# One hybrid-attention encoder layer on one core: the split of two heads' sum a step later, small loads moved up, later norms in halves, MLP squares stored a step later

## The chip, the cores and the metric

The kernel runs on one core of one Trainium2 chip. The core has five engines with an instruction stream each: TensorE (PE in the profile; its weight loads are listed as PEld), VectorE (DVE), ScalarE (ACT), GpSimd (POOL) and SyncE (SP), which here only issues DMAs. The metric is the device time of one execution in microseconds; three runs of the kernel before gave a median of 2637.62 us (2637.33 to 2642.32).

## The reference: what is computed

One layer, sequence 2048, width 1024, float32. Cut to what matters:

```python
mod = silu(c) @ w_ada + b_ada                      # six vectors of 1024: sh1 sc1 gt1 sh2 sc2 gt2
h = rmsnorm(x, g_norm1) * (1 + sc1) + sh1
q_sb, k_sb, v_sb, q_ca, k_ca, v_ca = split(h @ w_in)   # six pieces of 512 columns, 8 heads of 64 each
# stick-breaking attention (8 heads, strictly causal), z = q k / 8
w = sigmoid(z) * prod over the keys between s and t of (1 - sigmoid(z))     # from a running sum in the reference
o_sb = w @ v_sb
# chunked softmax attention (8 heads), own chunk of 64 and 8 chunks before it,
# q and k rms-normed per head, a learned relative bias
o_ca = softmax(q_ca k_ca / 8 + bias) @ v_ca
x = x + gt1 * (concat(o_sb, o_ca) @ w_o)
h = rmsnorm(x, g_norm2) * (1 + sc2) + sh2
x = x + gt2 * (square(relu(h @ w1)) @ w2)          # hidden width 4096
```

## The kernel before, in words

The sequence is reversed on the host and cut into four blocks of 512 tokens (`TB`); most tiles are 128 partitions by 512 float32. A product in full precision is made of two halves in a rounded format: every operand is split into a high part (ACT casts it) and a low part (DVE or POOL subtracts), and `mm3` issues three matmuls, high by high, high by low, low by high. Scratch tensors in DRAM (`scr_q`, `scr_k`, `scr_v`, `scr_w`, `scr_m`, `scr_hid`, `scr_s` and others) carry split operands from one stage to the next. Each engine runs its own instructions in the order in which the scheduler of the framework put them; most instructions go through a wrapper that keeps them in program order, and so have the line number of that wrapper, L42. SP's queue is in order as well: a store at its head that waits for a compute engine holds back the loads behind it.

**Start.** `load_x(3)`, the conditioning vector, the bias columns and `gcol[:, 0]` are loaded, then `load_first(k)` loads for each of eight k the three weight pieces (`wf`) and two rows of `w_ada` (`wa`). The loop `for k in range(KT)` prepares and multiplies k by k: the first three weight pieces by block 3, into six PSUM banks. After it the six results are stored (`store_qk`, tiles `stf`), and behind these stores come the loads of `gcol[:, 1]` (g_norm2) and of `gqk_sb` (the gains of the per-head norms).

**Projections.** `jobs` lists weight piece and block; `run_job` goes through its banks (8 times 3 matmuls each, tiles `pq` or `pt`) and calls `hook(job, n)` before each. The hooks do the norms of the other blocks: `start_norm` (squares and sums, then two later parts that make the rstd and multiply x, tile `xt`) and `end_norm(tb, ht)`, which for each of eight tiles adds the shift: ACT writes the high part of `ht`, DVE the low part. In hook ((0,3,3),1) DVE scales `gqk_sb` into `gqk_s`. Pieces 6 and 8 (q and k of the chunked heads) are normed per head: ACT squares a bank (`csq`), DVE reduces it (`cv`), POOL makes the power (`cy`), DVE scales the bank into `qh`, which frees the bank.

**Attention.** `units` lists (head, query block, key block) for the stick-breaking heads (class `SB`) and (head, query block) for the chunked heads (class `CA`), block 3 first, then 2, 1, 0, each block all SB heads and then all CA heads. A unit has four steps; the step loop runs with lag: the front unit's scores and weights at step i, the back unit's transposes and value products 8 steps (`LAG`) later. A step of an SB unit: PE makes `z`, ACT takes the sigmoid in place, DVE scans it into `p`, POOL subtracts neighbours into the weights `b`; the back unit's weights are transposed on PE (`wt`), split by ACT (`wth`) and DVE (`wtl`), and multiplied by `v` into `acc`. `z` and `wt` share four PSUM banks. `load(u)` brings q and k of a unit two units (`AHEAD`) before its first step, `load_values` its v. Two heads share one tile of 128 rows. At the end of a head `finish(u)` has ACT copy the two halves of `acc` into `otmp` and `o`; a list `soon` holds what is to be done one step later: `add`, in which POOL adds the halves, and after the second head of a pair, one more step later, `keep(u, o)`: ACT casts the sum `o` into the high part of `os`, POOL subtracts the low part, and SP stores `os` to `scr_m`.

Between the steps `fill` gives PE dense matmuls of a `Filler`: the projections that are still missing (`fill_qkv` for block 1, then 0; tiles `pf`, weights `fw` and `fv`), then the output projection (`outproj`, tiles `po`). A filler yields a float for a matmul, a callable for work on a finished bank, and "start" or "wait" once its first loads are issued; `RESTS` says for how many steps it then rests. The weight loads of the first filler are issued by its generator when the step loop first asks for work, after the last projection job.

**MLP.** Both products are made with seven instead of eight block products (Strassen-Winograd). `First` steps (7 products for each of 16 pairs of hidden tiles, of 12 matmuls each) form hidden tiles: relu and square on ACT, in `hidden` or, for product 2, in `run`, and each is stored at once to `scr_hid` by `keep(i, src)`; sums of squares (tiles `ca`, `cb`, `cv`, `ce`) are stored through `later.add(2, ...)`, two steps later. `second_sums` prepares sums of w2 (`w2s`, stored to `scr_s`). `Second` steps load pairs of hidden tiles and weights (`hw`), split them into `oph` and `opv`, and multiply.

Of the kernel before, what the change touches and what calls it, by code (L numbers as in the profile page):

```python
# [9 lines left out]
F32 = mybir.dt.float32  # L10
# [14 lines left out]
KT = D // P  # L25
# [54 lines left out]
def encoder_kernel(ctx, tc, xT, c, g1, g2, w_in, w_rest, gqk, bias, w_o, w1, w2, w_ada, b_ada, out):  # L80
    nc = tc.nc
    act, dve, pool, sp = nc.scalar, nc.vector, nc.gpsimd, nc.sync
    pe = Ordered(tc, nc.tensor)
    osp = Ordered(tc, nc.sync)
# [112 lines left out]
    def norm_apply(which, x, k, dst, pl, tg):  # L197

        j = 3 * which * KT + k
        a, b = aff[:, which, k : k + 1], mod[:, j : j + 1]  # L200
        hi, lo = dst[k][:, 0, :], dst[k][:, 1, :]
        act.activation(x, x, AF.Identity, scale=a, bias=b)
        act.copy(hi, x)
        return lambda: dve.tensor_tensor(lo, x, hi.bitcast(F32), op=ALU.subtract) and None
# [34 lines left out]
    if True:  # L239
# [228 lines left out]

            norms.add(wait, second)

        def end_norm(tb, ht):
            hts[tb] = ht
            for k, x in enumerate(xts[tb]):
                b = mod[:, k : k + 1]
                act.activation(ht[k][:, 0, :], x, AF.Identity, bias=b)
                dve.scalar_tensor_tensor(
                    ht[k][:, 1, :], x, b, ht[k][:, 0, :].bitcast(F32), op0=ALU.add, op1=ALU.subtract
                )
# [3 lines left out]
        def h_tile(tb):  # L482
            if tb % 2:
                return [hxp.tile([P, 2, TB], F32R, tag="hx", name=f"ht{tb}_{k}") for k in range(KT)]
            whole[tb] = hp.tile([P, KT, 2, TB], F32R, tag="hp", name=f"ht{tb}")
            return [whole[tb][:, k] for k in range(KT)]
# [10 lines left out]
        def load_first(k):  # L497
            if k % 2 == 0:
                wraw.append(ring.tile([P, 2, 3, CW], F32, tag="r8", name=f"wf{k}"))
            osp.dma_start(wraw[-1][:, k % 2], w_in[0:3, :, k, :].rearrange("g p c -> p g c"))  # L500
            for j in (KT + k, k):
                adas[j] = adaw.tile([P, D], F32, tag="wa", name=f"wa{j}")
                osp.dma_start(adas[j], w_ada[j * P : (j + 1) * P, :])
# [51 lines left out]
        for k in range(KT):  # L555
            if k + 2 < KT:
                load_first(k + 2)
            rest = norm_apply(0, xts[3][k], k, hts[3], np_, "a3") if k else None
            for j in (KT + k + 1, k + 1) if k + 1 < KT else ():
                ada_column(j, adas[j])  # L560
                if rest:
                    rest = rest()
            if rest:
                rest()
            if k + 1 < KT:
                first_scale(k + 1)
            if k + 2 < KT:
                first_w(k + 2)
            if k + 4 < KT:
                first_x(k + 4)  # L570
            if k == KT - 3:
                load_raw(*loads.pop(0), osp)
                load_x(2, osp)
            if k == KT - 1:
                for m in range(4):
                    weight_parts((0, 3), m)
            for m, p in enumerate(first):
                hi, lo = [w2s[k // 2][:, k % 2, l] if p == 2 else wide[:, k, l, p] for l in range(2)]
                for n in range(2):
                    cl = slice(n * P, (n + 1) * P)  # L580
                    mm3(
                        pss[2 * m + n], hi[:, cl], lo[:, cl], hts[3][k][:, 0, :], hts[3][k][:, 1, :],
                        k == 0, k == KT - 1,
                    )
# [3 lines left out]
        for m, p in enumerate(first):  # L588
            for n in range(2):
                grp, hf = divmod(p, 2)  # L590
                store_qk(grp, 0, pss[2 * m + n], stage(f"f{p}_3_{n}"), hf * 2 + n, 3)
        osp.dma_start(gcol[:, 1, :], g2)
        osp.dma_start(gqk_sb, gqk)

        todo = [(1.5, lambda j=j: ada(j)) for j in range(2 * KT, 6 * KT)]
        for i in range(NH):
# [5 lines left out]
        def hook(job, n):  # L602

            if (job, n) == ((0, 3, 3), 1):
                dve.tensor_scalar_mul(gqk_s[:, 0:1], gqk_sb[:, 0:1], 0.125)
                dve.tensor_copy(gqk_s[:, 1:2], gqk_sb[:, 1:2])
                for p in range(2):
                    sp.dma_start(scr_w[p,], wide[:, :, :, p, :].bitcast(F32))
            if (job, n) == ((0, 6, 3), 2):
                norms.flush()  # L610
                end_norm(2, h_tile(2))
            if (job, n) == ((0, 6, 2), 1):
                load_x(1)
            if (job, n) == ((0, 4, 3), 0):
                start_norm(1, 5, 3)
            if (job, n) == ((0, 10, 2), 0):
                norms.flush()
                end_norm(1, h_tile(1))
                load_x(0)
                behind.add(2, lambda: start_norm(0, 3, 2))  # L620
            if (job, n) == ((1, 6, 1), 2):
                norms.flush()
                end_norm(0, h_tile(0))
            if (job, n) == ((1, 6, 0), 1):
                sp.dma_start(scr_h, whole[0].bitcast(F32))

# [36 lines left out]
    if True:  # L663
# [36 lines left out]
        def finish(u):  # L700
            r = (u.h % 2) * HD
            q = HD - r
            if u.h % 2 == 0:
                pend["o"] = op.tile([P, TB], F32, tag="o", name=f"o{u.nm}")
            o = pend["o"]
            tmp = op.tile([P, TB], F32, tag="otmp", name=f"otmp{u.nm}")
            rows = slice(r, r + HD)
            act.copy(tmp[rows, :], u.acc[q : q + HD, :])
            act.copy(o[rows, :], u.acc[rows, :])

            def add():
                pool.tensor_tensor(o[rows, :], o[rows, :], tmp[rows, :], op=ALU.add)
                if u.h % 2:
                    soon.append(lambda: keep(u, o))

            soon.append(add)

# [187 lines left out]
            def weights(self, qi, kb):  # L905
                return self.ws[qi][:, (kb - qi) * P : (kb - qi + 1) * P]

        RESTS = {"wait": 4, "start": 3}
        resident = {}
        svs = []  # L910
        turn = [0]
# [39 lines left out]
        def fill_qkv(self, tb, ht, pieces):  # L951
# [3 lines left out]

            def narrow_load(piece, i):
                w = ring.tile([P, KT // 2, 2, CW], F32R, tag="r8", name=f"fw{tb}_{piece}_{i}")
                sp.dma_start(w.bitcast(F32), scr_w[piece,][:, i * 4 : i * 4 + 4, :, :])
                return {i * 4 + k: w[:, k] for k in range(KT // 2)}

            def wide_load(piece, k, n):
# [212 lines left out]
        AHEAD = 2  # L1174
        for u in units[:AHEAD]:
            load(u)
        run_job(len(jobs) - 1)
        units[0].scores(0)
        later.flush()
# [74 lines left out]
    if True:  # L1254
# [136 lines left out]
        class First(Step):  # L1391
# [43 lines left out]
            def run(self):  # L1435
# [19 lines left out]
                if i == 2:  # L1455
                    d["c11"] = kept(f"y{nm}")
                    act.activation(d["c11"], ps, AF.Relu)
                    act.activation(d["c11"], d["c11"], AF.Square)
                    self.keep(1, d["c11"])
                if i == 3:  # L1460
                    c12 = self.hidden(column_sum(dve, d["v"], ps, d["v"], ALU.add))

# [17 lines left out]
            def hidden(self, c, i=None):  # L1480
                act.activation(c, c, AF.Relu)
                act.activation(c, c, AF.Square)
                if i:
                    self.keep(i, c)
                return c

            def keep(self, i, src):
# [275 lines left out]
```

## Time and profile before

| what | value |
|---|---|
| three runs | 2637.33, 2637.62, 2642.32 us (median 2637.62) |
| the profiled execution's own time | 2637.35 us |
| its span, first to last instruction | 2635.6 us |
| its mean granted TensorE clock | 0.997 |
| PE busy | 2570.9 us, 98% of the span |
| DVE, ACT, POOL busy | 1876.8, 1409.5, 937.4 us (71%, 53%, 36%) |
| DMA | 650.68 MB, mean 247 GB/s |

How to read it: the profile is of one execution. Times in the views are microseconds from the span's start. A view of waits gives the engine and the tile of the instruction that waited, who released it, the total, how many times, and the longest. A row of the timeline gives start, length, engine, operation, output and inputs, count, and in square brackets the idle time of the engine before it and what ended that. A view of stretches gives the busy time of each engine in a stretch, the granted clock, and the share of the 16 DMA engines' time in use. In tile names the buffer numbers are left out: `z<-z` stands for every score tile. The stages: start and projections to about 422 us, attention to about 1345 us, the rest of the output projection to about 1420 us, the MLP to the end.

### The profile page before, as it was taken

How to read it: one execution, taken by the hardware profiler on the slowest of the kernel's cores; microseconds unless marked ns; L12 is line 12 of the kernel's file. 1: busy time of each engine (PE TensorE's matmuls, PEld its weight loads, DVE VectorE, ACT ScalarE, POOL GpSimd, SP SyncE). 2: the span in 40 equal slices, each digit the busy share in tenths (PEclk: the TensorE clock that was granted, in tenths of full speed). 3: DMA queues.
4: the chain of work that ended last, by engine and by line, in shares of the span. 5: the costliest groups of instructions: out<-in, count | busy, mean ns of one | idle time of the engine just before them, and what ended most of it. 6: DMA issues, size and time to landing. Idle time of an engine off the chain costs nothing. (4 is left out here: it accounts for less than half of the span.)

```text
span 2635.6 us, 39336 instructions
## 1 busy us (share of the span) xinstructions
PE 2570.9 (98%) x12528; PEld 2131.0 (81%) x12528; DVE 1876.8 (71%) x3233; ACT 1409.5 (53%) x2721; POOL 937.4 (36%) x1256
## 2 busy tenths in 40 slices
PE   7999999899999999999999999999999999999999
PEld 6788887777877888787888888888888888888887
DVE  7656766688788878998768777668856666555555
ACT  6333434766766677666754444466544454444443
POOL 4330145666666667766623232100002232200000
PEclk9999999999999999999999999999999999999999
DMA  9779878979976798755787777786764434375574
GB/s 348 289 305 361 333 297 287 286 227 296 304 220 215 242 277 262 253 188 194 208 313 259 275 256 270 258 311 219 255 228 168 168 140 162 129 256 192 200 268 155
DMA packets 257519, 650.68 MB, mean 247 GB/s; under 512 B 29472, under 2 KB 53024, under 8 KB 248224
## 3 DMA queue, kind: packets, MB, share of 16 engines
q1 hardware_dynamic: 256016, 643.45, 71.2%
q10 hardware_dynamic: 1296, 4.72, 0.4%
q8 instruction: 99, 1.62, 0.3%
q14 instruction: 108, 0.88, 0.1%
HBM read 456.69 MB, written 191.37 MB: 246 GB/s over the span
## 5 line engine op out<-in xcount | busy, mean ns | idle before, releaser
L42 PE MATMUL ps<-oph,opv 128*128 128x512 f32 x2688 | 612.3, 389 | 1.5 <-ACT opv L42 1.3
L42 PE MATMUL ps<-h,opw 128*128 128x512 f32 x2664 | 604.5, 389 | 1.6 <-DVE cx L42 1.6
L42 PEld LDWEIGHTS ps<-oph,opv 128*128 128x128 f32 x2688 | 503.8, 188 | 108.1 <-ACT opv L42 2.1
L42 PEld LDWEIGHTS ps<-h,opw 128*128 128x128 f32 x2664 | 499.9, 188 | 105.9 <-DVE cx L42 2.1
L42 POOL TENSOR_TENSOR b<-p 128x512 f32<-128x512 f32 (+1 forms) x320 | 291.9, 912 | 189.0 <-DVE p L42 112.4
L42 ACT CAST wth<-wt 128x512 fp32r<-128x512 f32 (+3 forms) x544 | 256.9, 483 | 169.2 <-PE wt L42 157.2
L42 DVE TENSOR_TENSOR wtl<-wt,wth 128x512 fp32r<-128x512 f32 (+3 forms) x544 | 290.1, 544 | 62.1 <-ACT wth L42 60.5
L42 DVE TENSOR_TENSOR oph<-hw,oph 128x512 fp32r<-128x512 f32 x224 | 155.1, 693 | 220.6 <-ACT oph L42 220.6
L42 PE MATMUL pt<-w,ht 128*128 128x512 f32 x1248 | 291.4, 393 | 4.9 <-DVE w L42 2.7
L42 ACT CAST oph<-hw 128x512 fp32r<-128x512 f32 x224 | 139.3, 622 | 282.2 <-PE ps L42 266.2
L42 POOL TENSOR_TENSOR ts<-w 128x512 f32<-128x512 f32 x32 | 45.1, 1410 | 663.9 <-DMA w<-in_w_dram 561.0
L42 PEld LDWEIGHTS pt<-w,ht 128*128 128x128 f32 x1248 | 234.5, 189 | 54.2 <-DVE w L42 3.0
L42 DVE TENSOR_TENSOR_SCAN p<-z,p,zero 128x512 f32<-128x512 f32 x192 | 245.8, 1280 | 43.7 <-ACT z L42 36.4
L42 PE MATMUL acc<-wth,v 128*128 128x512 f32 (+3 forms) x544 | 220.8, 410 | 0.0
L42 PE MATMUL z<-k,q 128*128 128x512 f32 (+3 forms) x640 | 187.7, 375 | 23.7 <-DVE p L42 19.1
L42 ACT ACTIVATE z<-z 128x512 f32<-128x512 f32 (+1 forms) x320 | 166.2, 520 | 57.6 <-PE z L42 54.0
L42 PE MATMUL acc<-wtl,v 128*128 128x512 f32 (+3 forms) x544 | 185.8, 348 | 0.0
L42 DVE TENSOR_TENSOR opw<-w,opw 128x512 fp32r<-128x512 f32 x127 | 98.2, 775 | 113.2 <-ACT opw L42 113.1
L42 POOL TENSOR_TENSOR e<-e,cols 128x640 f32<-128x640 f32 (+4 forms) x128 | 142.8, 1120 | 88.6 <-DVE cols L42 48.8
L42 PE MATMUL wt<-ident,b 128*128 128x128 f32 x1088 | 171.7, 273 | 1.0 <-DVE cols L42 0.3
L42 PEld LDWEIGHTS wt<-ident,b 128*128 128x128 f32 x1088 | 136.7, 141 | 42.3 <-DVE wtl L42 1.8
L42 PE MATMUL po<-fx,ow 128*128 128x512 f32 x576 | 162.3, 394 | 0.0
(194 smaller groups left out, 4081.1 us busy)
## 6 DMA issues: line engine op xcount, KB each, us to landing
hw<-scr_hid SPq DMA_DIRECT2D x112, 512.0 KB, 4.3
k<-scr_k SPq DMA_DIRECT2D x272, 128.0 KB, 4.3
v<-scr_v SPq DMA_DIRECT2D x136, 256.0 KB, 3.8
q<-scr_q SPq DMA_DIRECT2D x128, 256.0 KB, 5.2
w<-in_w_dram SPq DMA_DIRECT2D x64, 512.0 KB, 5.3
hw<-scr_s SPq DMA_DIRECT2D x64, 512.0 KB, 4.6
wa<-in_w_ada_dram SPq DMA_DIRECT2D x48, 512.0 KB, 6.8
ow<-scr_wo SPq DMA_DIRECT2D x24, 1024.0 KB, 5.9
```

Of the source, the lines that this page charges most:

```text
L42: return lambda *x, **y: self.tc.keep_in_program_order(f(*x, **y))
```

## The change

Seven edits, none of which changes what is computed:

1. The loads of `gcol[:, 1]` and `gqk_sb` go from behind the first six stores into the start loop, at k = 1, behind `load_first(3)`.
2. `end_norm` takes a range of tiles. For blocks 2 and 0 it is called for tiles 0 to 3 in the hook where it was called for all, and for tiles 4 to 7 in the hook of the next bank. Block 1 stays whole.
3. `keep` of a pair of heads is put on the list `soon` a second time, so that it is done one step later.
4. The first filler's two weight loads (`fw`, 1 MB each) are issued ahead of the last projection job, on the queue in program order.
5. `RESTS["start"]` goes from 3 to 0: the first filler no longer rests three steps.
6. Of the MLP's hidden tiles, the stores of product 2's square (`c11`) and of the two squares that `hidden` stores go to `later.add(2, ...)`.
7. `narrow_load` uses `ldq` instead of `sp`; during the step loop both are the same queue.

```diff
-        def end_norm(tb, ht):
+        def end_norm(tb, ht, *ks):
             hts[tb] = ht
-            for k, x in enumerate(xts[tb]):
-                b = mod[:, k : k + 1]
+            for k in range(*ks or (KT,)):
+                x, b = xts[tb][k], mod[:, k : k + 1]
                 act.activation(ht[k][:, 0, :], x, AF.Identity, bias=b)
                 dve.scalar_tensor_tensor(
                     ht[k][:, 1, :], x, b, ht[k][:, 0, :].bitcast(F32), op0=ALU.add, op1=ALU.subtract
...
             if k + 2 < KT:
                 load_first(k + 2)
+            if k == 1:
+                osp.dma_start(gcol[:, 1, :], g2)
+                osp.dma_start(gqk_sb, gqk)
...
                 store_qk(grp, 0, pss[2 * m + n], stage(f"f{p}_3_{n}"), hf * 2 + n, 3)
-        osp.dma_start(gcol[:, 1, :], g2)
-        osp.dma_start(gqk_sb, gqk)
...
             if (job, n) == ((0, 6, 3), 2):
                 norms.flush()
-                end_norm(2, h_tile(2))
+                end_norm(2, h_tile(2), 0, KT // 2)
+            if (job, n) == ((0, 6, 3), 3):
+                end_norm(2, hts[2], KT // 2, KT)
...
             if (job, n) == ((1, 6, 1), 2):
                 norms.flush()
-                end_norm(0, h_tile(0))
+                end_norm(0, h_tile(0), 0, KT // 2)
+            if (job, n) == ((1, 6, 1), 3):
+                end_norm(0, hts[0], KT // 2, KT)
...
                 if u.h % 2:
-                    soon.append(lambda: keep(u, o))
+                    soon.append(lambda: soon.append(lambda: keep(u, o)))
...
-        RESTS = {"wait": 4, "start": 3}
+        RESTS = {"wait": 4, "start": 0}
...
-                sp.dma_start(w.bitcast(F32), scr_w[piece,][:, i * 4 : i * 4 + 4, :, :])
+                ldq.dma_start(w.bitcast(F32), scr_w[piece,][:, i * 4 : i * 4 + 4, :, :])
...
         for u in units[:AHEAD]:
             load(u)
+        for _ in range(2):
+            filler[0].load()
         run_job(len(jobs) - 1)
...
                     act.activation(d["c11"], d["c11"], AF.Square)
-                    self.keep(1, d["c11"])
+                    c11 = d["c11"]
+                    later.add(2, lambda: self.keep(1, c11))
...
                 act.activation(c, c, AF.Square)
                 if i:
-                    self.keep(i, c)
+                    later.add(2, lambda: self.keep(i, c))
                 return c
```

What this makes of the order of instructions, at three places.

ACT in the attention of block 0, where the front unit is head 6: `os_5_0_3` is the split of heads 4 and 5 in block 0, `o_4_0_3` their sum, `z_6_0_3_1` the sigmoid of head 6, key block 3, second step. Before:

```order
L42 ACTIVATE z_6_0_3_1_14900<-z_6_0_3_1_14900 128x512
L42 CAST wth_6_0_1_2_14917<-wt_6_0_1_2_14906 128x512
L42 CAST os_5_0_3_14921<-o_4_0_3_14465 128x512
L42 ACTIVATE z_6_0_3_2_14927<-z_6_0_3_2_14927 128x512
L42 CAST wth_6_0_1_1_14946<-wt_6_0_1_1_14935 128x512
L42 ACTIVATE z_6_0_3_3_14952<-z_6_0_3_3_14952 128x512
```

The same place in the change:

```order
L42 ACTIVATE z_6_0_3_1_14900<-z_6_0_3_1_14900 128x512
L42 CAST wth_6_0_1_2_14917<-wt_6_0_1_2_14906 128x512
L42 ACTIVATE z_6_0_3_2_14923<-z_6_0_3_2_14923 128x512
L42 CAST wth_6_0_1_1_14942<-wt_6_0_1_1_14931 128x512
L42 CAST os_5_0_3_14946<-o_4_0_3_14465 128x512
L42 ACTIVATE z_6_0_3_3_14952<-z_6_0_3_3_14952 128x512
```

The cast of the sum stands one step later, behind that step's sigmoid and split.

DVE in the norm of block 2: `ht` is its low part, `qh_6_3_0` the scaling that frees the first bank of piece 6, block 3. Before:

```order
L42 SCALAR_TENSOR_TENSOR ht_940<-xt_3_601,mod,ht_940 128x512
L42 SCALAR_TENSOR_TENSOR ht_940<-xt_4_603,mod,ht_940 128x512
L42 SCALAR_TENSOR_TENSOR ht_940<-xt_5_605,mod,ht_940 128x512
L42 SCALAR_TENSOR_TENSOR ht_940<-xt_6_607,mod,ht_940 128x512
L42 SCALAR_TENSOR_TENSOR ht_940<-xt_7_609,mod,ht_940 128x512
L42 TENSOR_TENSOR qh_6_3_0_982<-pt_6_3_0_847,cy_6_3_0_877 128x512
```

In the change:

```order
L42 SCALAR_TENSOR_TENSOR ht_940<-xt_3_603,mod,ht_940 128x512
L42 TENSOR_TENSOR qh_6_3_0_974<-pt_6_3_0_847,cy_6_3_0_877 128x512
L42 TENSOR_REDUCE cv_6_3_2_978<-csq_6_3_2_976 128x8
L42 TENSOR_SCALAR cv_6_3_2_978<-cv_6_3_2_978 128x8
L42 SCALAR_TENSOR_TENSOR ht_940<-xt_4_605,mod,ht_940 128x512
L42 SCALAR_TENSOR_TENSOR ht_940<-xt_5_607,mod,ht_940 128x512
L42 SCALAR_TENSOR_TENSOR ht_940<-xt_6_609,mod,ht_940 128x512
```

The scaling goes ahead of the last four low parts.

SP around the last projection job: `scr_k` and `scr_v` are stores of that and the earlier job, `q_2_3` and `k_2_3_3` the loads of the third attention unit, `fw_2_0` and `fw_2_1` the first filler's weights. Before (`fw_2_0` stands eleven rows ahead of this piece):

```order
L42 DMA k_1_3_3_3747<-scr_k_3_0_120 64x512 x2
L677 DMA q_2_3_3949<-scr_q_3_1_89 64x1024 x2
L376 DMA scr_v_1_0_142<-sv_4_1_0_0_3777 128x4x256
L376 DMA scr_v_1_1_143<-sv_4_1_0_1_3778 128x4x256
L219 DMA scr_k_0_0_124<-st_8_0_0_3821 128x2x512
L219 DMA scr_k_0_1_125<-st_8_0_1_3830 128x2x512
L685 DMA k_2_3_3_3952<-scr_k_3_1_121 64x512 x2
L219 DMA scr_k_0_2_126<-st_8_0_2_3870 128x2x512
L219 DMA scr_k_0_3_127<-st_8_0_3_3879 128x2x512
L958 DMA fw_2_1_3966<-scr_w_222 128x2048
L376 DMA scr_v_1_0_142<-sv_4_1_2_0_3859 128x4x256
L376 DMA scr_v_1_1_143<-sv_4_1_2_1_3860 128x4x256
```

In the change:

```order
L42 DMA fw_2_0_3750<-scr_w_222 128x2048
L42 DMA fw_2_1_3752<-scr_w_222 128x2048
L376 DMA scr_v_1_0_142<-sv_4_1_0_0_3781 128x4x256
L376 DMA scr_v_1_1_143<-sv_4_1_0_1_3782 128x4x256
L219 DMA scr_k_0_0_124<-st_8_0_0_3825 128x2x512
L219 DMA scr_k_0_1_125<-st_8_0_1_3834 128x2x512
L219 DMA scr_k_0_2_126<-st_8_0_2_3874 128x2x512
L219 DMA scr_k_0_3_127<-st_8_0_3_3883 128x2x512
L376 DMA scr_v_1_0_142<-sv_4_1_2_0_3863 128x4x256
L376 DMA scr_v_1_1_143<-sv_4_1_2_1_3864 128x4x256
L682 DMA q_2_3_3953<-scr_q_3_1_89 64x1024 x2
L690 DMA k_2_3_3_3956<-scr_k_3_1_121 64x512 x2
```

Both weight loads stand ahead of the stores of the last job, and the third unit's q and k behind them.

## The prediction

> **What bounds the kernel now.** I read the page first, then PE's waits, then the timeline at each long one.
>
> ```profile
> span 2635.6 us, 39336 instructions
> PE 2570.9 (98%) x12528; PEld 2131.0 (81%) x12528; DVE 1876.8 (71%) x3233; ACT 1409.5 (53%) x2721; POOL 937.4 (36%) x1256
> ...
> L42 PE MATMUL ps<-oph,opv 128*128 128x512 f32 x2688 | 612.3, 389 | 1.5 <-ACT opv L42 1.3
> ```
>
> PE has the same matmuls before and after, so what can be gained is where PE stands idle (2635.6 - 2570.9 = 64.7 us) or runs at a lower clock. The last row is the MLP's largest group of dense matmuls: 612.3 / 2688 = 0.23 us each when they follow one another. PE's waits, us in total, times, longest:
>
> ```profile
> PE z L42 <- DVE p L42: 19.1, 25, 2.4
> PE cz L42 <- DMA k<-scr_k: 4.9, 2, 2.5
> PE pt L42 <- DVE w L42: 2.7, 1, 2.7
> PE pt L42 <- DVE qh L42: 2.2, 2, 1.1
> ```
>
> The largest that is not the start is the attention's: score matmuls that wait for DVE's scan to free a PSUM bank. Twelve of its longer cases follow one pattern, here the longest (idle time and its end in brackets):
>
> ```profile
> 1208.16 1.29 POOL L42 TENSOR_TENSOR r<-r,sq 128x512 f32<-128x512 f32 x1
> 1209.52 1.28 POOL L42 TENSOR_TENSOR o<-o,otmp 64x512 f32<-64x512 f32 x1
> 1210.84 0.62 ACT L42 CAST os<-o 128x512 fp32r<-128x512 f32 x1 [3.61 <-POOL o L42]
> 1212.04 1.28 DVE L42 TENSOR_TENSOR_SCAN p<-z,p,zero 128x512 f32<-128x512 f32 x1 [2.70 <-ACT z L42]
> 1213.38 1.22 PE L42 MATMUL z<-k,q 128*128 128x512 f32 x2 [2.41 <-DVE p L42]
> ```
>
> POOL runs behind, so its sum `o` is late; ACT, in order, stands 3.61 us at the cast of `o` with the next sigmoid behind it; DVE stands 2.70 us for the sigmoid; PE 2.41 us for DVE. This is what the third edit touches.
>
> **Part by part**, against the profiled execution's own 2637.35 us (its span and 1.75 us around it; 0.27 under the median of 2637.62).
>
> *Small loads.* SP, DVE and PE near 70 us, then two stretches (busy us and count of PE, PEld, DVE, ACT, POOL; granted clock; DMA share; GB/s):
>
> ```profile
> 59.07 0.33 SPq L42 DMA_DIRECT2D gcol<-in_g_dram  x1
> 62.30 0.33 SPq L42 DMA_DIRECT2D gqk_sb<-in_gqk_dram  x1
> 70.18 0.15 DVE L42 TENSOR_SCALAR gqk_s<-gqk_sb 128x1 f32<-128x1 f32 x1 [5.29 <-DMA gqk_sb<-in_gqk_dram]
> 71.05 4.21 PE L42 MATMUL pt<-w,ht 128*128 128x512 f32 x9 [2.73 <-DVE w L42]
> ...
> 69.40:76.30 6.90, 5.25 (x12) 4.13 (x13) 5.69 (x12) 0.00 (x0) 0.35 (x1) 0.51 1.08 387
> 76.30:83.20 6.90, 6.90 (x32) 5.67 (x31) 1.55 (x3) 0.60 (x1) 3.71 (x9) 1.00 1.08 408
> ```
>
> The DMA engines are full (share 1.08), so an 8-byte-a-partition load sits behind six stores for some 8 us; DVE waits 5.29 us for it with eight weight splits behind, and PE waits 2.73 us for the splits. Then it works 5.25 us at a granted clock of 0.51, which costs half of that, 2.6 us. Issued in the start loop, the load is there 30 us early; the eight splits can follow ACT's casts. Gain 2.7 + 2.6 = 5.3 us. Bounds: 2.7 if the low clock has another cause, 5.3 if all goes.
>
> [...]
>
> In the start loop two issues (0.33 us each, rows above) now stand ahead of later weight loads, 0.7 us. What covers that:
>
> ```profile
> 49.66 0.69 DVE L42 TENSOR_TENSOR ht<-xt,ht 128x512 fp32r<-128x512 f32 x1 [1.94 <-ACT ht L42]
> 52.07 1.52 PE L42 MATMUL pq<-ht,wfirst 128*128 128x512 f32 x6
> ```
>
> The last operand is ready at 50.35, PE takes it at 52.07: 1.7 us of slack, so I count nothing; without it the cost would be 0.7.
>
> *Norms in halves.* Two waits of PE, behind these two runs of DVE:
>
> ```profile
> 85.93 5.35 DVE L42 SCALAR_TENSOR_TENSOR xt<-xt,aff,pra 128x512 f32<-128x512 f32 x8
> 91.19 5.38 DVE L42 SCALAR_TENSOR_TENSOR ht<-xt,mod,ht 128x512 fp32r<-128x512 f32 x8
> 97.32 0.47 PE L42 MATMUL pt<-w,ht 128*128 128x512 f32 x1 [1.05 <-DVE qh L42]
> 327.68 0.70 PE L42 MATMUL pt<-w,ht 128*128 128x512 f32 x2 [1.11 <-DVE qh L42]
> ```
>
> The scaling `qh` that frees PE's bank now stands four low parts earlier, 4 x 0.67 = 2.7 us, more than the waits of 1.05 and 1.11. The other four come some 1.3 us later (`qh` and a reduction, two more passes of such a size), but PE needs the fifth tile only twelve matmuls into its next bank, 12 x 0.23 = 2.8 us. Gain 2.2, bounds 1.1 and 2.2.
>
> *The split of the sum.* ACT's waits from 510 to 1345 us, then the 4 us from the end of each of 13 waits, first, last and sum (12 of the view's 13, of which the last, at 1340.7, has PE busy behind it, and one at 539.3 that the view puts to a DMA):
>
> ```profile
> ACT os L42 <- POOL o L42: 26.5, 13, 3.6
> 539.30:543.30 4.00, 2.94 (x15) 2.01 (x14) 2.76 (x4) 3.83 (x8) 3.74 (x6) 1.00 0.15 61
> ...
> 1210.80:1214.80 4.00, 1.59 (x4) 1.16 (x4) 2.76 (x3) 2.78 (x6) 3.74 (x7) 0.76 0.15 61
> sum 52.00, PE 39.09 PEld 28.61 DVE 36.39 ACT 41.74 POOL 47.71; mean PE 3.01 PEld 2.20 DVE 2.80 ACT 3.21 POOL 3.67
> 1212.90:1216.30 3.40, 2.92 (x8) 2.33 (x9) 3.40 (x5) 1.14 (x3) 2.81 (x6) 0.50 0.59 199
> ```
>
> PE is idle 52.00 - 39.09 = 12.9 us in them, and 2.92 us at a clock of 0.50 behind the longest cost 1.5 more. POOL's additions stay where they are. Attention's 923 us over 456 steps make 2.0 us a step, and ACT's waits average 26.5 / 13 = 2.0: a cast that comes a step later mostly finds its sum ready. In the longest case 3.6 - 2.0 = 1.6 us of wait would be left, of which 3.61 - 2.41 = 1.2 never reached PE: 0.4. POOL's own subtraction moves a step too, and its load is unchanged (47.71 of 52 us busy here). DVE's scan could have started at 1209.3, when it ended its previous work. Late next would be ordinary scan waits: PE waits for `p` 22 times there, 16.7 us in all, 3.8 outside the 13 cases. I take 14.4 - 0.4 = 14.0; below, 7, if POOL's lag shifts half of the waits to the step after.
>
> Behind `keep` stands the store to `scr_m`, now a step later in SP's queue, with one or two loads moved ahead of it. Loads run two units, eight steps, ahead; I count nothing.
>
> *First filler early.* Two waits at the start of attention go when dense matmuls stand between the first scores:
>
> ```profile
> 424.01 0.41 PE L42 MATMUL z<-k,q 128*128 128x128 f32 x2 [0.84 <-DVE sv L42]
> 425.28 0.73 PE L42 MATMUL z<-k,q 128*128 128x512 f32 x2 [0.86 <-DVE p L42]
> 402.00 1.23 SPq L677 DMA_DIRECT2D q<-scr_q  x2
> 419.59 0.59 SPq L958 DMA_DIRECT2D fw<-scr_w  x1
> 424.00:510.00 86.00, 75.31 (x423) 62.22 (x424) 57.68 (x147) 59.15 (x149) 58.98 (x98) 0.98 0.98 305
> ```
>
> But from 424 to 510 the DMA engines are in use at 0.98: this stretch lasts as long as its transfers, and PE's 10.7 us idle there are mostly that, the two waits of ACT in it included. Of its transfers, 1 MB (`fw`, 128x2048) leaves and 0.75 MB (q and k of the third unit, 64x1024 and 64x512 twice each; q was issued at 402) comes in; nearly even. What stays is that six more dense matmuls are done by the same step: 6 x 0.23 = 1.4 us. I take 1.3; below, -2, if the third unit's q and k arrive late; above, 6, if PE's own waits were the limit.
>
> *MLP stores.* SP, ACT and PE near the end of the first `First` stage:
>
> ```profile
> 1688.20 0.45 SPq L42 DMA_DIRECT2D txn<-scr_x  x1
> 1692.92 0.32 SPq L42 DMA_DIRECT2D scr_hid<-cu  x1
> 1695.27 0.45 SPq L42 DMA_DIRECT2D hw<-scr_hid  x1
> 1700.66 0.62 ACT L42 CAST oph<-hw 128x512 fp32r<-128x512 f32 x1 [7.29 <-DMA hw<-scr_hid]
> 1706.89 3.06 PE L42 MATMUL ps<-h,opw 128*128 128x512 f32 x12 [1.63 <-DVE cx L42]
> 1719.39 1.31 PE L42 MATMUL ps<-oph,opv 128*128 128x512 f32 x3 [1.28 <-ACT opv L42]
> ```
>
> SP stands from 1688.65 to 1692.92 at the store of `cu`, with the load of `hw` behind it; ACT and DVE then stand for `hw`. The store of `cu` goes behind the load, but those of `ca`, `cb` and `cv`, sums that DVE has ready at nearly the same time, stay ahead. So `hw` comes about 0.9 us earlier, not 4. Gain 0.9 of the two waits' 2.9; bounds 0 and 2.9. In the rest of the MLP PE has no wait to lose.
>
> **Sum:** 5.3 + 2.2 + 14.0 + 1.3 + 0.9 = 23.7; 2637.35 - 23.7 = 2613.65, and 0.3 to the median: 2614.
>
> **Rivals.**
> (a) POOL is the next limit: it is 92% busy in the 13 stretches, and half of PE's waits only move a step. For it, POOL's late sum is the root; against it, the same work per two steps. Third term 7: 2621.
> (b) The half clock is not the stalls' doing and stays: terms 2.7 and 12.5 in place of 5.3 and 14.0, 2618. [...] The two rows of 0.51 and 0.50, each behind a stall of 2.4 us or more, speak against it.
> (c) Slower: SP's queue. Each of 32 stores to `scr_m` now lets its successors wait up to a step longer; 32 x 2.0 = 65 us if nothing hides it. The gains of 23.7 are gone when over a third of that reaches PE, that is, when loads have less than one step of their eight in hand, as between 424 and 510 they have. With half of it: 2614 + 32 = 2646. Against it, after 510 no wait of PE is for a transfer.
> (d) It does not do what it says: ACT's wait moves along with the cast, since POOL falls further behind. Third term 0: 2628, still faster.
>
> **Chances.** Forecast 0.62 (its own range 2609 to 2618), (a) 0.16, (b) 0.07, (c) 0.03, (d) 0.04; 0.05 for more (the crowded stretch and the MLP waits gone wholly, 4.7 + 2.0 more: 2607, and below), 0.03 for no change at all. The range 2604 to 2626 leaves out (c), (d), no change and the far end of more. A measurement of this kernel can tell about 0.2%, 5.3 us, from none. Faster by over that: all but (c), no change and a rest, 0.93; within 0.04; slower 0.03.
>
> **What would show it.** Right: no idle of DVE for `gqk_sb`, no clock under 1.00 near 70 us; no ACT wait for `o` after 510; PE's waits for `p` near 4 us; PE still waiting for k between 430 and 500; the `hw` load about 0.9 us behind its former lead. Wrong: ACT's waits for `o` still over 10 us; new waits of PE for q or k after 510; a new PE wait in the start loop.

## The result, and the profile after

| what | before | after |
|---|---|---|
| runs taken with the changed kernel | 2637.33 to 2645.11 us, median 2638.35 (5) | 2620.05 to 2629.01 us, median 2625.16 (5) |
| ratio | 1 | 0.9945 (0.9930 to 0.9961) |
| profiled execution | 2637.35 us, span 2635.6 | 2628.16 us, span 2626.5 |
| mean, before from its runs beside the experiments | 2641.2 us (45) | 2625.3 us (5) |

The changed kernel is faster by 13.2 us by its own set of runs, by 15.9 against the 45 runs of before that were taken beside the experiments. The forecast was 23.7 us less, 2614; 2625.16 lies in its range, near the upper end. The two traces show less of the gain than the runs do: the profiled execution of before is one of its faster ones (2637.35 against a mean of 2641.2), that of the changed kernel one of its slower ones (2628.16 against 2625.3).

The page of the changed kernel:

```profile
span 2626.5 us, 39315 instructions
...
PE 2569.7 (98%) x12528; PEld 2134.4 (81%) x12528; DVE 1885.4 (72%) x3233; ACT 1411.5 (54%) x2721; POOL 938.5 (36%) x1256
```

PE's idle time went from 64.7 to 56.8 us. DVE is busy for 8.6 us more, though it has the same 3233 instructions: some of them take longer than before, which becomes important below.

PE's waits after, in total, times, longest:

```profile
PE cz L42 <- DMA k<-scr_k: 8.1, 3, 5.9
PE z L42 <- DMA k<-scr_k: 6.7, 4, 3.0
PE z L42 <- DVE p L42: 6.0, 13, 1.1
...
PE ps L42 <- DVE cx L42: 3.9, 2, 3.7
...
PE ps L42 <- ACT cu L42: 1.4, 4, 0.4
```

The wait for DVE's `p`, outside the start the largest of before at 19.1 us, has shrunk to 6.0. The waits for `k` have grown from 4.9 and 1.7 to 8.1 and 6.7, and the MLP has waits for `cx` and `cu`. PE's wait for `w` near 70 us (2.7) and its two waits for `qh` (2.2) are gone.

To find where time came and went, I took the end of the same PE instruction in two traces and call the difference to the profiled execution of before the *lead* (us; "534" is the score matmul that ended there in before):

| kernel | at 422 | at 534 | last score, 1243 | first `ps<-h,opw`, 1409 | end |
|---|---|---|---|---|---|
| after | 7.5 | -0.8 | 17.4 | 16.4 | 9.2 |
| without edit 6 | 8.3 | 3.1 | 21.3 | 19.0 | 16.1 |
| without edits 4, 5, 7 | 8.1 | 3.4 | 20.9 | 19.8 | 11.0 |
| without edit 3 | 7.5 | -2.0 | -4.4 | -4.5 | -11.3 |
| edits 1, 2 | 6.6 | 4.1 | 5.4 | 5.4 | 2.6 |
| edits 1, 2, 3 | 7.2 | 3.5 | 21.1 | 20.2 | 17.3 |
| light (fewer transfers) | 7.4 | 9.1 | 27.3 | 26.3 | 21.5 |
| nosum (no sums on POOL) | 8.0 | 1.5 | 18.6 | 17.6 | 20.1 |
| edits 1, 2, 3, `hw` early | 7.9 | 3.6 | 21.2 | 20.4 | 22.2 |

So the changed kernel wins 7.5 us before 422, loses 8 in the early attention, wins 18 in the rest of it, loses 1 up to the MLP and 7 in it. The two gains were forecast; the losses were not. The rows below the first are the experiments.

**Start.** DVE near 65 us:

```profile
64.65 0.14 DVE L42 TENSOR_SCALAR gqk_s<-gqk_sb 128x1 f32<-128x1 f32 x1
```

and two stretches that answer to those around 70 us before, in the columns of the prediction's stretches:

```profile
62.00:68.90 6.90, 6.90 (x36) 5.86 (x35) 6.69 (x13) 6.27 (x12) 0.00 (x0) 1.00 1.04 417
68.90:75.80 6.90, 6.90 (x32) 5.68 (x31) 2.99 (x7) 0.60 (x1) 1.81 (x5) 1.00 1.07 382
```

No idle time ahead of `gqk_s`, no idle PE, and a granted clock of 1.00 where 0.51 stood.

**Attention from 510 on.** ACT's wait for the sum, and PE's for the scan, in that stretch:

```profile
ACT os L42 <- POOL o L42: 3.9, 5, 1.5
...
PE z L42 <- DVE p L42: 5.6, 12, 1.1
```

Before, these were 26.5 us in 13 waits and 16.7 us in 22.

**The crowded stretch.** PE, then SP, in the changed kernel:

```profile
485.36 0.47 PE L42 MATMUL acc<-wth,v 128*128 128x512 f32 x1 [1.32 <-DMA v<-scr_v]
485.67 0.40 PE L42 MATMUL acc<-wtl,v 128*128 128x512 f32 x1
491.96 1.19 PE L42 MATMUL cz<-k,q 128*128 128x512 f32 x2 [5.90 <-DMA k<-scr_k]
...
474.24 0.45 SPq L972 DMA_DIRECT2D fw<-scr_wv  x1
474.74 1.00 SPq L972 DMA_DIRECT2D fv<-scr_wv  x1
475.79 1.07 SPq L699 DMA_DIRECT2D v<-scr_v  x1
476.96 1.30 SPq L972 DMA_DIRECT2D fw<-scr_wv  x1
478.31 1.33 SPq L682 DMA_DIRECT2D q<-scr_q  x2
479.68 1.23 SPq L690 DMA_DIRECT2D k<-scr_k  x2
```

The whole stretch, and two pieces of it, after:

```profile
424.00:534.00 110.00, 92.93 (x516) 77.51 (x515) 66.67 (x189) 76.05 (x193) 69.46 (x106) 0.92 0.92 264
...
450.10:456.80 6.70, 5.57 (x18) 4.83 (x19) 2.70 (x3) 1.64 (x3) 3.44 (x7) 0.50 1.03 345
487.70:497.80 10.10, 5.83 (x19) 5.07 (x20) 2.02 (x7) 1.37 (x4) 2.49 (x3) 0.50 0.75 210
```

and the whole stretch before:

```profile
424.00:534.00 110.00, 96.83 (x546) 79.72 (x547) 72.77 (x199) 78.89 (x202) 75.91 (x119) 0.98 0.94 286
```

The `k` for which PE waits 5.90 us was issued at 479.7, behind three loads of filler weights, and landed 12 us later. From within the two longest of these waits, 3.0 and 5.9 us, the granted clock was 0.50: for 6.8 us from 450.0 and 10.2 us from 487.6, where the profile of before has one of 3.4 us in this stretch.

**MLP.** DVE and POOL in one step of the first product (the same four POOL sums, the same passes of DVE), before:

```profile
1458.09 0.69 DVE L42 TENSOR_TENSOR opw<-w,opw 128x512 fp32r<-128x512 f32 x1 [1.87 <-ACT opw L42]
1458.70 0.68 DVE L42 TENSOR_TENSOR w2s<-w2s 128x512 f32<-128x512 f32 x1
1459.76 1.32 DVE L42 TENSOR_TENSOR opw<-ts,opw 128x512 fp32r<-128x512 f32 x1 [0.38 <-ACT opw L42]
1461.01 1.77 DVE L42 TENSOR_TENSOR w2s<-w2s 128x512 f32<-128x512 f32 x1
1462.71 0.68 DVE L42 TENSOR_TENSOR cv<-ps,cv 128x512 f32<-128x512 f32 x1
...
1458.92 1.62 POOL L42 TENSOR_TENSOR ts<-w 128x512 f32<-128x512 f32 x1 [13.28 <-DMA w<-in_w_dram]
1462.20 1.74 POOL L42 TENSOR_TENSOR w<-w 128x512 f32<-128x512 f32 x1
```

and after:

```profile
1443.06 1.36 DVE L42 TENSOR_TENSOR opw<-w,opw 128x512 fp32r<-128x512 f32 x1 [1.87 <-ACT opw L42]
1444.34 1.78 DVE L42 TENSOR_TENSOR w2s<-w2s 128x512 f32<-128x512 f32 x1
1446.04 1.77 DVE L42 TENSOR_TENSOR opw<-ts,opw 128x512 fp32r<-128x512 f32 x1
1447.74 1.77 DVE L42 TENSOR_TENSOR w2s<-w2s 128x512 f32<-128x512 f32 x1
1449.43 0.68 DVE L42 TENSOR_TENSOR cv<-ps,cv 128x512 f32<-128x512 f32 x1
...
1442.57 1.30 POOL L42 TENSOR_TENSOR ts<-w 128x512 f32<-128x512 f32 x1 [11.97 <-DMA w<-in_w_dram]
```

In these rows a DVE pass with both inputs in SBUF that started while POOL was in one of its sums took 1.32 to 1.78 us instead of 0.68. Before, POOL began 0.8 us behind the pass at 1458.09, and two passes were slow; after, it began 0.5 us ahead of it, and four were. Between 1420 and 1700 us 32 of DVE's additions and subtractions were slow (over 0.9 us) before, and 40 after: 6.9 us more in all. Of the stores that the sixth edit moved, that of `cu` stands in SP's queue ahead of the `w1` loads of these steps (tile `w`). Before:

```profile
1449.61 0.32 SPq L42 DMA_DIRECT2D scr_hid<-cu  x1
1450.02 0.38 SPq L42 DMA_DIRECT2D scr_hid<-ca  x1
1451.98 1.03 SPq L42 DMA_DIRECT2D w<-in_w_dram  x2
```

and after:

```profile
1433.85 0.32 SPq L42 DMA_DIRECT2D scr_hid<-ca  x1
1435.59 0.41 SPq L42 DMA_DIRECT2D scr_hid<-cu  x1
1436.83 0.91 SPq L42 DMA_DIRECT2D w<-in_w_dram  x2
```

The store of `cu` stood first, with the other stores and the `w1` loads behind it; now it stands behind those of `ca`, `cb` and `cv`. DVE falls behind PE by its slow passes, and PE meets it at the end of the stage. DVE's `ca` before:

```profile
1691.48 0.68 DVE L42 TENSOR_TENSOR ca<-cv,cy 128x512 f32<-128x512 f32 x1
```

DVE, SP, ACT and PE at the same place after:

```profile
1682.57 0.68 DVE L42 TENSOR_TENSOR ca<-cv,cy 128x512 f32<-128x512 f32 x1
...
1685.47 0.45 SPq L42 DMA_DIRECT2D hw<-scr_hid  x1
...
1690.89 0.62 ACT L42 CAST oph<-hw 128x512 fp32r<-128x512 f32 x1 [6.44 <-DMA hw<-scr_hid]
...
1697.13 1.22 PE L42 MATMUL ps<-h,opw 128*128 128x512 f32 x2 [3.67 <-DVE cx L42]
```

and the stretch from 1695.9:

```profile
1695.90:1702.70 6.80, 5.57 (x13) 4.41 (x14) 4.30 (x7) 4.59 (x8) 0.00 (x0) 0.50 0.95 300
```

The wait was 1.63 us before and is 3.67 now, and PE's 5.57 us of work at a clock of 0.50 behind it cost 2.8 us more, estimated as half of it from these two numbers.

### The profile page after: what moved, and what is told of

Same layout as the page of the kernel before. It is cut to its first block, busy times and chain, and to the rows that moved or that the text cites. A ratio compares the mean times of both kernels' runs of the same rounds, so it can differ in the third digit from the quotient of the medians.

```text
span 2626.5 us, 39315 instructions
## 1 busy us (share of the span) xinstructions
PE 2569.7 (98%) x12528; PEld 2134.4 (81%) x12528; DVE 1885.4 (72%) x3233; ACT 1411.5 (54%) x2721; POOL 938.5 (36%) x1256
## 5 line engine op out<-in xcount | busy, mean ns | idle before, releaser
L42 DVE TENSOR_TENSOR opw<-w,opw 128x512 fp32r<-128x512 f32 x127 | 106.6, 841 | 113.2 <-ACT opw L42 113.1
```

The source lines that it names most:

```text
L42: return lambda *x, **y: self.tc.keep_in_program_order(f(*x, **y))
```

## The experiments

Twelve runs were made, of ten kernels (two ran twice). All ratios are to runs of before that were taken along with the kernel, in three sets (medians of before 2639.97, 2641.58 and 2643.03 us).

**1. Without the sixth edit** (no6): the stores at once, all else as changed.

```diff
-                    c11 = d["c11"]
-                    later.add(2, lambda: self.keep(1, c11))
+                    self.keep(1, d["c11"])
...
-                    later.add(2, lambda: self.keep(i, c))
+                    self.keep(i, c)
```

> The change without the sixth edit: the MLP's squares are stored at once again. Against the kernel before, the changed one loses 7.2 us between 1392 us and its end in the two profiles. Theory A (the later stores move SP's queue, the w1 loads land sooner against DVE, POOL's sums run beside more of DVE's passes, and DVE, slowed, falls behind PE): this loss goes, DVE has about 32 slowed passes between 1420 and 1700 as before, not 40, no idle of PE over 3 us near 1697, and the time is about 2618. Rival (the loss is the scatter of one execution, or comes with the shifted phase from the attention): still some 7 us lost behind 1392, 2625.

Measured: 2620.64 us (2618.38 to 2621.36), ratio 0.9917 (0.9903 to 0.9931). The MLP loses 2.9 us of lead instead of 7.2; DVE has 36 slow passes, halfway between 32 and 40. A wait of 3.1 us for `cx` at 1691 stays, so one expectation of theory A missed. The sixth edit costs the changed kernel some 4.5 us, and a second cause for the wait at the end of the stage had to be found.

**2. Without edits 4, 5 and 7** (no45): the first filler late, with its rest, and `sp` in the narrow load.

```diff
-        RESTS = {"wait": 4, "start": 0}
+        RESTS = {"wait": 4, "start": 3}
...
-        for _ in range(2):
-            filler[0].load()
```

> The change without edits 4, 5 and 7: the first filler loads late and rests three steps, as before. Against before, the changed kernel loses 9.9 us between 422 and 530 us. Theory A (the two weight loads of 1 MB, issued early, take the full DMA engines from q, k and v): the loss goes, about -8 at 530 against before, and the time is about 2615. Rival B (the stores to scr_m, a step later in SP's queue, hold the loads behind them): the loss stays with the third edit, about +1 to +3 at 530, 2625.

Measured: 2625.84 us (2621.79 to 2627.85), ratio 0.9938 (0.9924 to 0.9952), as the changed kernel. At 534 the lead is 3.4, neither kept at 8 (theory A) nor gone (rival B). Both theories fell as stated: the early loads are at most a part of the loss there.

**3. Without the third edit** (no3):

```diff
-                    soon.append(lambda: soon.append(lambda: keep(u, o)))
+                    soon.append(lambda: keep(u, o))
```

> The change without the third edit: the split of two heads' sum one step earlier, as before. All of the 19.8 us won between 530 and 1345 should go, since the waits of ACT for the sum come back (26 us in 13 waits). Between 422 and 530, theory A (early weight loads) keeps the loss of 10: about 2645, slower than before. Rival B (the later stores to scr_m) gives it back: about 2635.

Measured: 2644.0 us (2640.24 to 2648.69), ratio 1.0012 (1.0003 to 1.0021). ACT's wait is back in the trace, from 510 to 1345 us:

```profile
ACT os L42 <- POOL o L42: 23.1, 13, 3.6
```

Without this one line the six other edits together are no gain. Theory A's number came out; but it came from more than the early loads, as experiment 5 shows.

**4. Edits 1, 2 and 3 alone** (e123, and again as e123b in the last set): the changed kernel with the diffs of experiments 1 and 2 together.

> Edits 1, 2 and 3 alone: no early filler, stores of the MLP at once. Theory A: neither loss is there, so 2638 less 7.5 (start and projections) less 20 (attention behind 530), about 2610, faster than the changed kernel by some 15. Rival B: the crowded stretch loses with the third edit, about 2618. If both losses are scatter: 2625, as the changed kernel.

Measured: 2618.95 us (2616.63 to 2620.06), ratio 0.9910 (0.9894 to 0.9926): faster than the changed kernel by 6 us, not by 15. It is nearly rival B's number; whether its cause holds, experiment 5 tells. DVE has 34 slow passes.

**5. Edits 1 and 2 alone** (e12): that, and the diff of experiment 3 besides.

> Edits 1 and 2 alone. All kernels with them reach the attention 7.2 to 8.3 us ahead of before, and those without the early filler are only 3.4 us ahead at 534 us. Theory C (between 424 and 530 the transfers set the pace, so that PE, coming earlier, only waits longer for k, and runs at half clock behind these waits): the lead shrinks to about 3.5 here too, with some 10 us of half clock in the stretch instead of 3.4; 2635 to 2637 in all. Rival B (the third edit's later stores to scr_m cost the 4 us): the lead of 7 is kept, 2631.

Measured: 2634.68 us (2629.94 to 2640.41), ratio 0.9976 (0.9965 to 0.9987). The trace has theory C's lead, 4.1 at 534, and its half clock, 13.7 us from the first score to 534 (10.2 of them after 424) against 3.4 in the profile of before. But PE does not wait longer there: its idle time from the first score to 534 is 12.7 us, and was 14.0. So rival B is out, since the lead shrinks without the third edit too, and C is right about the clock and wrong about more waiting; the median is just under C's range and 3.7 over B's number. And in time the two edits bring the full 6 to 7 us: the mean of 12 runs is 2634.2, against 2641.2. So the lead that seems lost at 534 is probably in good part the profile of before, an execution with little half clock in this stretch; no second trace of before was kept that could show it. The number of such stretches goes with much of the scatter from run to run (last section).

**6. Half of the fillers' weight loads** (light): leaves half of each filler weight out, as its expectation says.

```diff
-                ldq.dma_start(w.bitcast(F32), scr_w[piece,][:, i * 4 : i * 4 + 4, :, :])
-                return {i * 4 + k: w[:, k] for k in range(KT // 2)}
+                ldq.dma_start(w[:, 0:2].bitcast(F32), scr_w[piece,][:, i * 4 : i * 4 + 2, :, :])
+                return {i * 4 + k: w[:, k % 2] for k in range(KT // 2)}
...
-                sp.dma_start(w.bitcast(F32), scr_wv[piece // 6,][:, k : k + n])
-                return {k + i: w[:, i] for i in range(n)}
+                sp.dma_start(w[:, 0:1].bitcast(F32), scr_wv[piece // 6,][:, k : k + 1])
+                return {k + i: w[:, 0] for i in range(n)}
```

> The change, with the block fillers' weight loads halved: half of each narrow load, and one k instead of two in the wide ones, each tile's first part used twice (the projections of blocks 1 and 0 are not the reference's). The same matmuls, some 4 MB fewer transfers beside the early attention. Theory C (transfers set the pace from 424 to 530): PE's waits for k there go (14 us in the changed kernel), no half clock there, and the lead of 7 us at 424 is kept or grown at 534; about 10 us less in all, 2615. Rival (SP's order, with stores that wait for their engine ahead of the loads, sets it): waits for k of over 3 us stay and the time stays within 4 us of 2625.

Measured: 2616.34 us (2615.89 to 2619.21), ratio 0.9915 (0.9899 to 0.9930), 9 us under the changed kernel. The lead at 534 is 9.1, half clock in the stretch 3.4 us. PE's waits there:

```profile
PE cz L42 <- DMA k<-scr_k: 6.6, 3, 4.1
PE z L42 <- DMA k<-scr_k: 2.7, 3, 1.2
```

and the stretch:

```profile
424.00:534.00 110.00, 96.99 (x557) 80.75 (x556) 73.39 (x201) 82.94 (x207) 77.45 (x118) 0.98 0.92 262
```

Theory C's time came out: fewer transfers make this stretch shorter. Its other signs came only in part: waits for `k` stay at 9.3 us in all, one of them over 3 us, as the rival said, and one length of half clock is left. And the amount is not all. From the first score to the matmul at 534, before moves 32.1 MB in 112.3 us, the changed kernel 31.6 MB in 120.5 us, with the DMA engines in use at 0.94 and 0.91, and light 29.3 MB in 110.6 us. So the 8 us between before and the changed kernel are not more transfers; what holds the same transfers back there, their order in SP's queue or the half clock of PE, was not tried by itself.

**7. Without POOL's sums** (nosum): leaves the sums out, as its expectation says.

```diff
-                s1, s2, s4 = (temp(f"s{self.nm}_{n}") for n in (0, 1, 3))
-                s3 = d["21"]
-                column_sum(pool, s1, d["21"], d["22"], ALU.add)
-                column_sum(pool, s2, s1, d["11"], ALU.subtract)
-                column_sum(pool, s3, d["11"], d["21"], ALU.subtract)
-                column_sum(pool, s4, d["12"], s2, ALU.subtract)
-                d["S", 5], d["S", 6], d["S", 7], d["S", 3] = s1, s2, s3, s4
+                d["S", 5], d["S", 6], d["S", 7], d["S", 3] = d["21"], d["11"], d["22"], d["12"]
```

> The change without POOL's four sums of w1 blocks for each pair of hidden tiles: the operands of four products are the w1 blocks themselves (the MLP's first product is not the reference's). Theory D (the sixth edit brings the w1 loads, and so POOL's sums, on top of DVE's passes, which then take 1.3 to 1.8 us instead of 0.68, and DVE falls behind PE): no slowed pass of DVE between 1420 and 1700, no wait of PE for cu, the wait at 1697 (3.7 us and 3.4 of lost clock) gone or under 1.5, 2617 to 2619. Rival (the hidden tile's load for the second product, late in SP's queue, makes that wait): it stays at 3 us or more, 2623 to 2625.

Measured: 2618.94 us (2616.40 to 2623.16), ratio 0.9923 (0.9908 to 0.9938). PE's only wait from 1420 to 1720:

```profile
PE ps L42 <- ACT opv L42: 1.2, 1, 1.2
```

No slow pass of DVE is left (0 of 292), none of the waits for `cu`, none for `cx`. Theory D's signs all came: with the sixth edit in place, and without POOL beside DVE, the MLP loses nothing. But this takes away more than the sixth edit brought: the lead grows by 2.5 us in the MLP, where the changed kernel loses 7.2 and no6, without the sixth edit, still 2.9. So it shows that POOL's sums make the loss, and not how much of it is the sixth edit's; the kernel without sums and without the sixth edit was not run.

**8. The first `hw` load one step earlier** (hw8, and again as hw8b), on edits 1, 2 and 3:

```diff
-                at(n - 7, steps[n].load)
+                at(n - (8 if n == begin + 7 * NP else 7), steps[n].load)
```

> Edits 1, 2 and 3 with the first hidden tile of the second product loaded one step earlier, ahead of the three stores that wait for DVE. In edits 1 to 3 alone PE waits 3.19 us at 1689 and loses 1.7 us to a half clock: DVE stands for ACT, ACT for this load. If this load is the cause: both go, 2618.95 - 4.9 = about 2614, the fastest yet. If DVE's lag behind PE is the cause (theory D): the wait shrinks by under 1.5 us, 2617 to 2619.

Measured: 2616.29 us (2615.14 to 2618.05), ratio 0.9913 (0.9898 to 0.9928). That is 2.7 us under e123, between the two forecasts of 4.9 and under 1.5. From 1420 to 1720 PE has no wait left (in the trace of hw8b one of 0.7 us for `cu`), though DVE still has 34 slow passes. So the wait at the end of the stage needs both, DVE's lag and the late load, and goes when either goes.

**9. The last set**: edits 1, 2 and 3 again (e123b), with the early load (hw8b), with the early filler beside (hw8x45), and with the sixth edit instead (hw8x6). Their edits are those shown above.

> Edits 1, 2 and 3 again, so that the next three are compared with it under one set of runs: 2617 to 2621.

> Edits 1, 2 and 3 with the first hidden tile's load a step earlier, again. The traces put 4.9 us on the wait and the half clock that it removes, one execution each; the medians, with different runs of before, 2.7. Theory (the load makes the wait): 2.5 to 5 us under edits 1 to 3 alone, that is 2614 to 2616. Rival (scatter): within 1.5 us of them.

> The same with the early first filler (edits 4, 5 and 7). So far its price at 534 us is about 3 in the traces (leads of 3.5 without it, 0.8 of loss to 3.1 of lead with it), but -0.7 and +1.7 in two pairs of medians. If the early 1 MB loads displace k: 1 to 3 us over the kernel without it. My forecast of -1.3 would be 1.3 under it.

> Edits 1, 2 and 3, the load a step earlier, and the sixth edit. Theory (the sixth edit makes DVE lag, and its lag reaches PE mainly where DVE also waits for that load): with the load early, of its 5 us only the small waits for cu are left, 1 to 2.5 us over the kernel without it. Rival (the lag reaches PE whatever the load does): 4 to 5 us over it.

Measured: e123b 2619.82 (2616.59 to 2622.83), ratio 0.9910 (0.9895 to 0.9925); hw8b 2617.28 (2613.55 to 2625.45), 0.9908 (0.9890 to 0.9925); hw8x45 2616.19 (2614.58 to 2618.94), 0.9902 (0.9887 to 0.9917); hw8x6 2621.16 (2618.29 to 2624.60), 0.9920 (0.9905 to 0.9934).

The early load is worth 2.5 us by these medians and 2.7 by those of the earlier sets, but the intervals overlap, and the ratios of the earlier sets (0.9913 with it, 0.9910 without) show no gain: shown in the trace, not settled in time. The early filler costs nothing that can be measured (-1.1; the other two pairs gave -0.7 and +1.7). The sixth edit costs 3.9 us by these medians even here, which is nearly its rival's number, though these two intervals overlap as well; its PE waits from 1420 to 1720:

```profile
PE ps L42 <- ACT cu L42: 2.5, 5, 0.8
PE ps L42 <- ACT opv L42: 0.7, 1, 0.7
```

The fastest version is hw8x45, edits 1 to 5 and 7 and the early `hw` load: faster than the changed kernel by some 9 us, but not told apart from hw8b.

## Why the prediction was right or wrong

In means over runs, against the 45 of before (2641.2): edits 1 and 2 bring 7.0 (12 runs, 2634.2); the third 15.2 more (11 runs of e123 and e123b, 2619.1); the sixth added to these three costs 6.5 (no45, 2625.5; the two other pairs of medians give 4.5 and 3.9); the early filler is about nothing. 7.0 + 15.2 - 6.5 = 15.7, and 15.9 is measured. The steps do not simply add: taken from the whole change, the third edit is worth 18.8 (no3, mean of 12 runs 2644.1).

*Small loads* (5.3) and *norms in halves* (2.2) were right in mechanism: 7.5 of lead at 422 and 7.0 in time. That 7.5 is exactly the sum is luck. By the same lead, read closer, the stall at 70 us brought 5.4 and the two places of `qh` 1.3 and 1.4, 2.7 in all; but at 45 us the changed kernel was 0.65 behind. Between 20 and 45 us the thirteen traces with the first edit lose 0.0 to 1.2, 0.65 in the mean, where the prediction counted nothing and named 0.7 as the price if the slack that it saw did not cover the two issues. The half clock went with the stall, so rival (b) is out at that place. For the change as a whole it must be said less strongly: the changed kernel's mean granted clock is 0.9966, that of before 0.9964, so the half clock that went at 70 and 1213 us came back elsewhere in others' waits.

*The split of the sum* (14.0) was right in mechanism and nearly in size: 15.2, or 18.8 by no3. Rivals (a), with 7, and (d), with 0, are out: ACT's waits after 510 went from 26.5 to 3.9 us, PE's for `p` to 5.6 (forecast: none and near 4). From 534 to the last score e123 takes 690.7 us and e12 706.9; 12.7 of these 16.2 us are idle time of PE, 12.5 of it waits for `p` between a matmul `acc<-wtl,v` and the next score. The rest lies mostly there too: counted from start to start, the time behind `acc<-wtl,v` falls by 14.2 us and that behind `z<-k,q` by 1.6. The profile models the ends of matmuls (the rows at 485.36 and 485.67 overlap by 0.16 us), so that the first part of such a gap can count as busy. Rival (c), SP's queue held by the later stores, has its place but not its price: e12, without the third edit, has at 534 nearly the same lead as e123, 4.1 and 3.5. Of the signs of being wrong, one came in small: after 510 the changed kernel has three waits for `k`, of 0.8, 0.8 and 0.6 us.

*First filler early* (1.3) was too hopeful by a little: 0 in time, and in the traces some 3 us lost between 422 and 534, where kernels with it (light aside) take 117.5 to 121.9 us and those without it 114.9 to 117.0 (before itself, without it too, 112.4); PE is idle for 17.3 to 19.2 us there with it and 12.7 to 15.6 without. That is near its lower bound of -2, which was for q and k that arrive late; in the changed kernel a score matmul waits 1.90 us for `k` at 423.5, and in the traces without the early loads none does there. The statement beside it, "this stretch lasts as long as its transfers", was borne out by experiment 6 only in part: fewer transfers shorten it, but the same transfers take 112 to 122 us.

*MLP stores* (0.9, bounds 0 and 2.9) is the step that failed, in its sign. Its working was right: `hw` was issued 3.8 us behind DVE's `ca` before (1695.27 and 1691.48) and 2.9 after (1685.47 and 1682.57), the forecast 0.9 earlier. What failed is the sentence "In the rest of the MLP PE has no wait to lose", and the lower bound of 0 that goes with it. I followed the moved stores only to the load behind them at one place. They stand ahead of the `w1` loads in every pair of hidden tiles too, and their new order lets those loads land a little earlier against DVE, so that POOL's sums more often begin ahead of the DVE pass that they used to follow. Of 13 pairs, POOL begins within 2.5 us of DVE's `cx` (the next pass comes at 2.55) in none or one without the sixth edit (eight traces), and in four to six with it (five); in the median POOL begins 2.67 to 2.77 us behind `cx` with it and 2.75 to 3.38 without. DVE's slow passes are 37 to 43 with it and 32 to 36 without, in the same thirteen traces. That the sixth edit costs time is shown (6.5 and 4.5 us, in two pairs clear of the scatter), and experiment 7 shows that the stage loses nothing once POOL's sums are gone; that the earlier landing of `w1` sets these against DVE is read from the counts, and was not tried by itself, for instance with a `w1` load held back.

The rest of the miss is the yardstick. I summed against one execution of 2637.35 and put its median 0.3 above. In 45 runs the mean of before is 2641.2, so 3.6 of the 11 us between 2614 and 2625 were never in the kernel: 2641.2 - 23.7 would have been 2617.5.

## What to carry to other kernels

When a store or load is moved, follow every queue position behind it through the whole loop, up to the engine that its successor sets going: here, as far as the counts above tell, a load that landed some tenths of a us earlier put two engines on top of each other in four to six of 13 pairs of hidden tiles, where it had been none or one. Work on an engine with slack (POOL, 36% busy) was not free here: it slowed passes of an engine that others wait for (DVE) from 0.68 us to a median of 1.77. A profiled execution is one draw: before a sum of small terms is set against it, ask where it lies among the runs, and which of its waits are there in every run.

## What was not expected of the hardware

DVE and POOL: of DVE's additions and subtractions between 1420 and 1700 us that began while POOL was in a sum, 32 of 35 with both inputs in SBUF were slowed before (the other three began at the very start of a sum or in its last 0.2 us) and 40 of 40 after, to a median of 1.77 us; of those with an input in PSUM (`cv<-ps,cv`), 0 of 14 and 0 of 7, at 0.68. The rows at 1462.71 and POOL's at 1462.20 show one. All 72 slowed passes of the two traces end 0.55 us behind the end of the POOL sum in which they began, as if they had been held until it was over.

The half clock: it comes in lengths of 3.4, 6.8 and 10.2 us, begins 1 to 5 us behind the start of an idle time, and a wait of 1.48 us was enough in e123, where PE came back at 429.53:

```profile
429.53 0.98 PE L42 MATMUL z<-k,q 128*128 128x512 f32 x2 [1.48 <-DMA k<-scr_k]
```

```profile
429.80:433.10 3.30, 3.30 (x12) 2.84 (x11) 1.40 (x2) 1.17 (x2) 0.47 (x1) 0.50 1.05 258
```

while in before one of 1.70 us at 436.93 had none behind it. So the length of a stall alone did not decide it; in the traces it goes with where the idle time falls. In each of the 14 traces all starts of a half clock lie on one grid of 3.413 us (in before 69.45, 499.53 and 1212.92, which are 126 and 209 steps apart). Of the windows of this grid between 52 and 2600 us that ran at full clock, 35 of 35 with 1.88 us or more of idle PE were followed by half clock, 14 of 29 with 1.49 to 1.88, 1 of 57 with 1.0 to 1.49, and none with less. The 1.48 of e123 and the 1.70 of before each fell into one window, in the band where both occur; seven stalls of 2.0 to 2.5 us, each divided between two windows (in before the one that ends at 490.98), cost no clock. About half of the scatter goes with the clock: over the 45 runs of before, time and mean granted clock have a correlation of -0.70, and the runs average 2636.5 us at a mean granted clock of 0.998 (6 runs), 2640.0 at 0.997 (17), 2642.3 at 0.996 (13), and 2645.0 at 0.995 or 0.994 (9).
